# Router logits from unnormalised residual sums, joined attention keys and two more expert tiles in a three-layer decoder kernel

## The chip, the core and the metric

The kernel runs on one core of a Trainium2 chip, as one launch. The metric is the device time of one execution in microseconds, as the median of the runs shown. The engines are named as in the profile: PE is TensorE's matrix product and PEld its load of weights, DVE is VectorE, ACT is ScalarE, POOL is GpSimd and SP is SyncE, which here only issues DMAs.

## The reference, cut to what matters

Two layers of a first block are followed by one layer of a second block; the change touches the first block alone. It has 512 latent tokens and 256 context tokens of width 1024. One layer, cut to the lines that the change computes in another way:

```python
def layer_norm(x, g, b):
    mu = mean(x); var = mean((x - mu)**2)
    return (x - mu) * rsqrt(var + 1e-6) * g + b
def modulate(x, shift, scale):
    return layer_norm(x) * (1 + scale) + shift

# window attention, per block i of 128 queries: key blocks i-1, i, i+1 (banded), the 256 context keys, a sink
s = concat([where(band, q @ k_window, -1e30), q @ k_context, sink])
o = softmax(s) @ concat([v_window, v_context])
...
x = layer_norm(ALPHA * x + g1 * (o @ w_out), ln1_g, ln1_b)
h2 = modulate(x, sh2, sc2)
x = layer_norm(ALPHA * x + g2 * ec_moe(h2, ...), ln2_g, ln2_b)

def ec_moe(h, w_router, w_gate, w_up, w_down):      # 16 experts, each takes its best 2*n/16 tokens
    aff = softmax(h @ w_router)
    g, idx = top_k(aff.T, cap)
    ye = (silu(xs @ w_gate) * (xs @ w_up)) @ w_down * g     # xs = h[idx]
```

In layer 0 the context tokens go through the same steps with weights of modulation of their own; in layer 1 (`last`) they only serve as keys.

## The kernel before, in words

All products are float32. Many are made exact enough by splitting an operand into a high part (`fp32r`) and a low part; those run as three or two products. A router product or a transpose runs as plain float32, and each of its matmul calls is two instructions on TensorE.

A layer has these stages. **Projections and convolution** (`gemm`, L433 on). **Attention** (L587 to L730): `units` yields 4 + 4 neighbourhood units (`unit_b`) and 16 window units (`unit_a`, 4 pairs of heads `g` by 4 query blocks `i`), and in layer 0 also context units (`unit_c`); `pipeline` lays the back half of one unit beside the front half of the next. `unit_a` (L644) makes the scores of two heads in one PSUM tile `S_` with `qk` (L601), which is one product with the high and one with the low part of the keys: the block before (128 columns), the context (256), then this block and the next (128 or 256). So for `i` of 1 and 2 a unit has 12 products, of which 4 have 128 columns; for `i` = 3 it has 12, of which 8 have 128; for `i` = 0 it has 8 of 256. `softmax` (L624) reads the scores with the mask `band`, and `finish` transposes and multiplies with the values.

**Output projection and routing** (L733 to L868). First come loads on SP's queue: residual rows `xn`, gates `g`, norm vectors `lng` and `lnb`, router weights `wr`. Then `wrs` = router weights times (1 + scale), and the **setup products** `lg` of the shift with `wr` (L765), 8 calls for each of the two kinds of tokens in layer 0 and 8 in layer 1. `token_tile(t)` (L805) is a generator for 128 tokens, with these steps: four halves of the output product (12 matmuls each), where VectorE adds the residual (L800, L801); the first norm (`ln_affine`, in place) and the second norm to `z2` with its store to `zd`; 8 transposes of `z2` (L833) to `ht`; 8 router calls `lg` (L838), L842 to L848 the softmax; the transpose `tk` (L851) into the row of affinities; and after tile 3 `topk` of the latents (L885 on, VectorE). Tiles 0 to 3 are latents, 4 and 5 (layer 0 alone) context. The loop at L859 interleaves them by hand: in round `u` it steps tiles `(u, u-2, u, u, u-1, u, u-1, u-2)`. From `u` = 4 on TensorE's instructions are held in that order (`pin`); elsewhere a planner at build time with a cost model orders each engine's instructions, earlier ones in the program first.

**Experts** (`moe`, L955 on). 192 weight tiles of 128 by 2048 (1 MB each) per layer stream through a ring: `RIGHT` tiles `mr` in memory that is free early, `RING` = 4 tiles `r` (also used by the output projection) and `MRING` tiles `m`. That makes 12 in layer 0 and 16 in layer 1. A load waits until the tile that it replaces has been read. Of the first use of the ring, loads 6 to 11 in layer 0 and 14 and 15 in layer 1 are held behind the first gathers on POOL's queue (L985 to L989). `gather` (L997) fetches an expert pair's tokens by an indirect DMA from `zd`, transposes and modulates them to `xt`. In layer 0 `product0` runs the latent half of the first gate product, within it `topk` and `gather` for the context, then the context half.

Of the kernel before, what the change touches and what calls it, by code (L numbers as in the profile page):

```python
# [11 lines left out]
F32R = mybir.dt.float32r  # L12
# [3 lines left out]
OP = mybir.AluOpType  # L16
AX = mybir.AxisListType
# [14 lines left out]
RIGHT = (1, 3)  # L32
# [28 lines left out]
class K:  # L61
# [179 lines left out]
    def layer(self, l):  # L241
# [25 lines left out]
        band = self.t(kvp, [P, 640], tag="band")  # L267
# [70 lines left out]
        else:  # L338
# [238 lines left out]
        ML = self.t(mixp, [P, KC, 768], F32R, tag="lo")  # L577
        self.MH, self.ML = MH, ML
# [63 lines left out]
        zero = band[:, 128:384]  # L642

        def unit_a(g, i, qs):  # L644

            c0, c1 = (256 if i == 0 else 128), (640 if i == 3 else 768)
            n = c1 - c0
            vt = ([i - 1] if i else []) + [4, 5, i] + ([i + 1] if i < 3 else [])
            pt = []
            for s in range(2):  # L650
                S_ = self.t(ps, [P, 1024], tag="S")
                if i:
                    qk(S_, qs[s], s, i * P, KHA, KLA, 128, (i - 1) * P, P)
                qk(S_, qs[s], s, i * P, KHA, KLA, 256, 512, 256)
                qk(S_, qs[s], s, i * P, KHA, KLA, 512, i * P, P if i == 3 else 2 * P)
                p = self.t(ap_, [P, 769], tag=f"p{s}", bufs=3)
                softmax(p, [(S_[:, c0:c1], band[:, c0 - 128 : c1 - 128], slice(0, n))], n, s, g)
# [94 lines left out]
        nc.sync.dma_start(wr, A["w_r"][l])  # L752
        aff = self.sT.rearrange("p k s -> p (k s)")
# [4 lines left out]

        wrs, rb = [], []
        for s in range(1 if last else 2):  # L760
            w = self.t(ecp, [P, KC, NE], tag=f"wrs{s}", bufs=1)
            nc.vector.tensor_tensor(w, wr, mt[:, s, 32:40].unsqueeze(2).broadcast_to([P, KC, NE]), op=OP.mult)
# [42 lines left out]
        def token_tile(t):  # L805
# [8 lines left out]
            x = XN[:, t, :]  # L814
            self.ln_affine(x, s2, lng, lnb, sm, z2, self.t(ps, [P, D], tag="junk", bufs=1), sx)
# [13 lines left out]
            ht = self.t(ecp, [P, KC, P], tag="ht")  # L829
            for k0 in (0, 4):  # L830
                tp = self.t(ps, [P, 512], tag="tr")
                for k in range(k0, k0 + 4):
                    pin(nc.tensor.transpose(tp[:, (k - k0) * P : (k - k0 + 1) * P], z2[:, k * P : (k + 1) * P], self.ident))  # L833
                (nc.vector.tensor_copy if k0 else nc.scalar.copy)(ht[:, k0 : k0 + 4, :].rearrange("p k f -> p (k f)"), tp)
            yield
            lg = self.t(ps, [P, NE], tag="lg", bufs=1)
# [4 lines left out]
            g = self.t(sm, [P, NE], tag="rg")  # L841
            nc.vector.tensor_tensor_reduce(out=g, in0=lg, in1=rb[s], scale=1.0, scalar=-3.0e38, op0=OP.add, op1=OP.max, accum_out=mx)  # L842
# [112 lines left out]
    def moe(self, l):  # L955
# [21 lines left out]
        def load(src):  # L977
# [7 lines left out]
            if (right + RING + 1, 14)[l] <= n < right + RING + xr:  # L985
# [122 lines left out]
        def up(p):  # L1108
# [9 lines left out]
            ht = self.t(mp, [P, KC, P], tag="hT")  # L1118
# [14 lines left out]
        def down(p):  # L1133
# [813 lines left out]
def constants():  # L1947
# [11 lines left out]
    C["bandm"] = np.concatenate([np.where(k >= q, 0.0, NEG), np.zeros((P, 384)), np.where(k <= q, 0.0, NEG)], 1).astype(np.float32)  # L1959
# [28 lines left out]
def layout(I):  # L1988
# [13 lines left out]
    H["ln_vec"] = np.stack([I["ln1_g"], I["ln1_b"], I["ln2_g"], I["ln2_b"]], 1)  # L2002
    H["w_r"] = c(I["w_router"].reshape(2, KC // 2, P, 2, NE).transpose(0, 2, 1, 3, 4).reshape(2, P, KC, NE))
# [55 lines left out]
```

## Time and profile before

| | us |
|---|---|
| median of 3 runs (2538.52 to 2540.21) | 2538.67 |
| the profiled execution | 2537.64 |
| its span, first to last instruction | 2535.9 |
| layer 0: attention, from about | 210 to 355 |
| layer 0: output projection and routing | 355 to 486 |
| layer 0: experts in full flow | 486 to 1016 |
| layer 1: attention, from about | 1205 to 1315 |
| layer 1: output projection and routing | 1315 to 1411 |
| layer 1: experts in full flow | 1411 to 1866 |
| second block | 1866 to 2536 |

The stages overlap a little; the borders are those at which the timelines change hands. A timeline row gives the start, the duration, the engine, the line of the kernel, the operation, output and inputs by name, the shape and the count, and in brackets for how long the engine had been idle and what ended that. L97 is the helper of all matmuls. A matmul's duration holds its passage through the array, so that the cost of one in a row of them is read from start to start. In the table of stages the granted clock of TensorE is a share of full speed (1.00 is 2.4 GHz, 0.50 is 1.2 GHz) and DMA is the mean busy share of 16 DMA engines.

### The profile page before, as it was taken

Reading aid. Unit: us, or ns where it says so; the run is one execution under the profiler, and the core shown is the slowest. Engines: PE = TensorE matmul, PEld = TensorE weight load, DVE = VectorE, ACT = ScalarE, POOL = GpSimd, SP = SyncE. Lnnn points to the kernel's source line nnn. Section 1 sums busy time; section 2 is a strip of 40 time slices with the busy share of each in tenths; the row PEclk is TensorE's granted clock in tenths of the full one; section 3 lists DMA queues with packets and bytes.
Section 4 is the critical chain, followed back from the end, with each engine's and each line's share of the span. In section 5 each row is a group of like instructions: output and inputs, shape, how many; then the busy total and the mean of one; then the engine's idle time right before and its main releaser. Section 6 shows DMA issues by size and latency. Waiting matters only on the chain. (4 is left out here: it accounts for less than half of the span.)

```text
span 2535.9 us, 36633 instructions
## 1 busy us (share of the span) xinstructions
PE 2379.5 (94%) x14806; PEld 1454.1 (57%) x14806; DVE 1080.2 (43%) x2379; ACT 701.5 (28%) x1398; POOL 450.6 (18%) x628
## 2 busy tenths in 40 slices
PE   6999899899999999699897899999989989999999
PEld 3776778333333333377776333333357878888887
DVE  6957766311011100685866112221157676423232
ACT  3225643100000000542752100000043375322221
POOL 4013422111011111311430000000033332101100
PEclk9999899899999999789998899999999999999999
DMA  9445032899999999543224999999953302123220
GB/s 355 147 158 193 1 134 99 322 409 406 397 375 383 374 392 391 187 173 130 79 93 193 375 423 422 424 423 423 424 230 123 105 18 93 67 83 111 105 84 33
DMA packets 96537, 593.20 MB, mean 234 GB/s; under 512 B 12912, under 2 KB 13936, under 8 KB 31600
## 3 DMA queue, kind: packets, MB, share of 16 engines
q1 hardware_dynamic: 84240, 549.62, 54.7%
q0 software_dynamic: 8384, 30.68, 3.7%
q10 hardware_dynamic: 3744, 10.56, 1.1%
q8 instruction: 116, 1.90, 0.3%
q14 instruction: 53, 0.43, 0.0%
HBM read 571.68 MB, written 19.14 MB: 233 GB/s over the span
## 5 line engine op out<-in xcount | busy, mean ns | idle before, releaser
L97 PE MATMUL mm<-m,xt 128*32 128x512 f32 (+1 forms) x2536 | 412.8, 595 | 0.0
L97 PEld LDWEIGHTS mm<-m,xt 128*32 128x32 f32 (+1 forms) x2536 | 126.8, 115 | 216.5 <-issue 212.7
L97 PE MATMUL mm<-r,xt 128*32 128x512 f32 (+1 forms) x1128 | 238.7, 598 | 0.0
L97 PE MATMUL mm<-m,hT 128*32 128x512 f32 (+1 forms) x792 | 174.8, 595 | 6.1 <-DMA m<-w_down 6.1
L97 PE MATMUL mm<-mr,xt 128*32 128x512 f32 (+1 forms) x432 | 138.6, 615 | 0.2 <-ACT xt L1015 0.2
L1123 ACT COPY hT<-tr 128x512 f32<-128x512 f32 x16 | 9.4, 587 | 446.4 <-PE tr L1122 446.4
L97 PEld LDWEIGHTS mm<-r,xt 128*32 128x32 f32 (+1 forms) x1128 | 69.6, 117 | 90.4 <-issue 86.1
L97 PE MATMUL mm<-r,hT 128*32 128x512 f32 (+1 forms) x560 | 118.7, 594 | 1.7 <-DMA r<-w_down 1.7
L1114 DVE TENSOR_TENSOR sg<-sg,mm 128x512 f32<-128x512 f32 x32 | 22.0, 688 | 212.3 <-PE mm L97 142.7
L1013 DVE TENSOR_SCALAR xt<-tr,modT 128x128 f32<-128x128 f32 (+1 forms) x96 | 36.1, 388 | 170.4 <-ACT xt L1015 168.9
L521 DVE SCALAR_TENSOR_TENSOR acc<-hp,cw,acc 128x798 f32<-128x798 f32 (+1 forms) x120 | 106.2, 912 | 2.6 <-ACT acc L518 0.9
L97 PEld LDWEIGHTS mm<-m,hT 128*32 128x32 f32 (+1 forms) x792 | 54.9, 121 | 88.1 <-issue 69.0
L97 PE MATMUL po<-dl,rh 128*128 128x512 f32 x256 | 99.2, 390 | 1.4 <-DVE dl L1277 1.4
L1155 DVE SCALAR_TENSOR_TENSOR yd<-mm,gp,g 128x512 f32<-128x512 f32 x18 | 13.5, 751 | 204.1 <-PE mm L97 203.2
L1000 POOL DMA_INDIRECT gat<-zd,ip x24 | 23.1, 960 | 435.6 <-PE tr L1008 404.3
L97 PE MATMUL px<-HH,uh 128*128 128x512 f32 x256 | 99.8, 390 | 0.7 <-ACT HH L1847 0.7
L97 PE MATMUL px<-HH,ul 128*128 128x512 f32 x256 | 100.1, 391 | 0.0
L97 PE MATMUL pv<-ptT,VN 128*64 128x128 f32 x1360 | 96.1, 286 | 4.2 <-DVE lo L622 2.1
L97 PE MATMUL px<-HL,uh 128*128 128x512 f32 x256 | 100.0, 390 | 0.0
L97 PE MATMUL po<-dh,rh 128*128 128x512 f32 x256 | 98.7, 390 | 0.0
L97 PE MATMUL po<-dh,rl 128*128 128x512 f32 x256 | 98.6, 390 | 0.0
L640 POOL TENSOR_SCALAR p<-p,rl 128x768 f32<-128x768 f32 (+2 forms) x96 | 79.6, 833 | 104.1 <-DVE rl L639 95.0
(531 smaller groups left out, 5201.7 us busy)
## 6 DMA issues: line engine op xcount, KB each, us to landing
m<-w_gate SPq DMA_DIRECT2D x79, 1024.0 KB, 18.4
m<-w_down SPq DMA_DIRECT2D x71, 1024.0 KB, 18.8
m<-w_up SPq DMA_DIRECT2D x62, 1024.0 KB, 17.4
r<-w_mod SPq DMA_DIRECT2D x48, 1024.0 KB, 6.0
r<-w_down SPq DMA_DIRECT2D x41, 1024.0 KB, 17.3
r<-w_up SPq DMA_DIRECT2D x40, 1024.0 KB, 13.0
r<-w_gate SPq DMA_DIRECT2D x31, 1024.0 KB, 13.7
mr<-w_up SPq DMA_DIRECT2D x20, 1024.0 KB, 19.8
```

The lines of the kernel that those rows point to most:

```text
L97: return self.nc.tensor.matmul(out, lhsT, rhs, start=start, stop=stop)
L521: lambda t=t: nc.vector.scalar_tensor_tensor(out=dst, in0=hp[c][:, t : t + n], scalar=cw[:, c, t : t + 1], in1=dst, op0=OP.mult, op1=OP.add)
L640: nc.gpsimd.tensor_scalar(p[:, :n], p[:, :n], rl, 0.0, op0=OP.mult, op1=OP.add)
L1000: nc.gpsimd.indirect_dma_start(out=g[0:n], out_offset=None, in_=self.zd[l][s], in_offset=bass.IndirectOffsetOnAxis(ap=self.route[s][2][0:n ...
L1013: nc.vector.tensor_scalar(o, i, sc, sh, op0=OP.mult, op1=OP.add)
L1114: nc.vector.tensor_tensor(apart(sg[:, c]), apart(sg[:, c]), paired(ux[n]), op=OP.mult)
L1123: (nc.vector.tensor_copy if k0 else nc.scalar.copy)(ht[:, k0 : k0 + 4, :].rearrange("p k s -> p (k s)"), tp)
L1155: nc.vector.scalar_tensor_tensor(out=y, in0=d, scalar=gp[:, p : p + 1], in1=G2[0][:, c], op0=OP.mult, op1=OP.mult)
```

## The change

- `unit_a` makes the scores of the window's blocks in one product of up to 384 columns instead of two, with the context's beside them in the other PSUM bank; `band` and the order of the values follow.
- The token tiles transpose the residual sums `XN` (step 5, ahead of the first norm) instead of `z2`. The router multiplies them with `w1` = `wr` (1 + scale) gain, and the two means and two inverse deviations enter on VectorE as four operations of 128 by 16 on the logits. For that the setup makes four vectors instead of one: 24 calls instead of 8 for each kind of tokens, with a new load `lnT` (64 bytes for each partition).
- The order in a round is `(u, u-2, u-1, u, u-1, u, u, u-2)`.
- Layer 1's ring has five `mr` tiles instead of three, 18 in all. All its loads are on SP's queue. The room comes from single buffers for `gat`, `hT`, `oh` and the split output weights in layer 1, from split weights laid into the unused end of `MH` and `ML`, and from `h` in `QA`.

```diff
-RIGHT = (1, 3)
+RIGHT = (1, 5)
...
         nc.vector.scalar_tensor_tensor(out=x, in0=tmp, scalar=rs, in1=b, op0=OP.mult, op1=OP.add, accum_out=o)
+        return nm, rs
...
-                    h = self.t(lnp, [P, 512], tag="h")
+                    h = QA[k % 2]
...
+        if last:
+            MH, ML = (x.rearrange("p k f -> p (k f)") for x in (MH, ML))
+            spare = MH[:, KC * W : KC * 768], ML[:, KC * W : KC * 768]
+            MH, ML = (x[:, 0 : KC * W].rearrange("p (k f) -> p k f", k=KC) for x in (MH, ML))
...
-            c0, c1 = (256 if i == 0 else 128), (640 if i == 3 else 768)
-            n = c1 - c0
-            vt = ([i - 1] if i else []) + [4, 5, i] + ([i + 1] if i < 3 else [])
+            w = list(range(max(0, i - 1), min(4, i + 2)))
+            vt = w + [4, 5] if i == 0 else [4, 5] + w
+            n = len(vt) * P
+            cc, cw_, cm = (512, 256, 384) if i == 0 else (256, 512, 0)
...
-                if i:
-                    qk(S_, qs[s], s, i * P, KHA, KLA, 128, (i - 1) * P, P)
-                qk(S_, qs[s], s, i * P, KHA, KLA, 256, 512, 256)
-                qk(S_, qs[s], s, i * P, KHA, KLA, 512, i * P, P if i == 3 else 2 * P)
+                qk(S_, qs[s], s, i * P, KHA, KLA, cc, 512, 256)
+                qk(S_, qs[s], s, i * P, KHA, KLA, cw_, w[0] * P, len(w) * P)
...
+        lnT = self.t(ecp, [P, 2, KC], tag="lnT", bufs=1)
+        nc.sync.dma_start(lnT, A["ln_T"][l])
...
-            lg = self.t(ps, [P, NE], tag="lg", bufs=1)
-            for k in range(KC):
-                self.mm(lg, mt[:, s, 24 + k : 25 + k].broadcast_to([P, P]), wr[:, k, :], k == 0, k == KC - 1)
+            nc.vector.tensor_tensor(w1, w0, lnT[:, 0, :].unsqueeze(2).broadcast_to([P, KC, NE]), op=OP.mult)
+            lg = self.t(ps, [P, 4 * NE], tag="lg", bufs=1)
+            for o, n, lh, rh in (
+                (0, 2, lambda k: one, w), (2, 1, lambda k: lnT[:, 1, k : k + 1], w0), (3, 1, lambda k: mt[:, s, 24 + k : 25 + k], wr),
+            ):
+                for k in range(KC):
+                    self.mm(lg[:, o * NE : (o + n) * NE], lh(k).broadcast_to([P, P]), rh[:, k, :], k == 0, k == KC - 1)
...
-            if i < 3:
-                wh = self.t(ecp, [P, 2048], F32R, tag="woh")
-                wl = self.t(ecp, [P, 2048], F32R, tag="wol")
+            if last and i == 1:
+                wh, wl = spare
+            elif i < 3:
+                wh, wl = (self.t(ecp, [P, 2048], F32R, tag=n, bufs=1 if last else 2) for n in ("woh", "wol"))
...
             yield from product(t, 1, s2)
+            yield
+            x = XN[:, t, :]
+            xt = x.rearrange("p (a k b) -> p a b k", b=2, k=P)
+            ht = self.t(ecp, [P, KC, P], tag="ht", bufs=1)
+            for k0 in (0, 4):
+                tp = self.t(ps, [P, 512], tag="tr")
+                for k in range(k0, k0 + 4):
+                    pin(nc.tensor.transpose(tp[:, (k - k0) * P : (k - k0 + 1) * P], xt[:, k // 2, k % 2, :], self.ident))
+                (nc.vector.tensor_copy if k0 else nc.scalar.copy)(ht[:, k0 : k0 + 4, :].rearrange("p k f -> p (k f)"), tp)
...
-            self.ln_affine(x, s2, lng, lnb, sm, z2, self.t(ps, [P, D], tag="junk", bufs=1), sx)
+            nm1, rs1 = self.ln_affine(x, s2, lng, lnb, sm, z2, self.t(ps, [P, D], tag="junk", bufs=1), sx)
...
-                    pin(nc.tensor.transpose(tp[:, (k - k0) * P : (k - k0 + 1) * P], z2[:, k * P : (k + 1) * P], self.ident))
...
+            cW, cG, cB, cS = rb[s]
+            g = self.t(sm, [P, NE], tag="rg")
+            nc.vector.scalar_tensor_tensor(out=g, in0=cG, scalar=nm1, in1=lg, op0=OP.mult, op1=OP.add)
+            nc.vector.scalar_tensor_tensor(out=g, in0=g, scalar=rs1, in1=cB, op0=OP.mult, op1=OP.add)
+            nc.vector.scalar_tensor_tensor(out=g, in0=cW, scalar=nm, in1=g, op0=OP.mult, op1=OP.add)
+            nc.vector.scalar_tensor_tensor(out=g, in0=g, scalar=rs, in1=cS, op0=OP.mult, op1=OP.add)
...
-            nc.vector.tensor_tensor_reduce(out=g, in0=lg, in1=rb[s], scale=1.0, scalar=-3.0e38, op0=OP.add, op1=OP.max, accum_out=mx)
+            nc.vector.tensor_reduce(mx, g, axis=AX.X, op=OP.max)
...
-            for t in (u, u - 2, u, u, u - 1, u, u - 1, u - 2):
+            for t in (u, u - 2, u - 1, u, u - 1, u, u, u - 2):
...
-            if (right + RING + 1, 14)[l] <= n < right + RING + xr:
+            if not last and right + RING + 1 <= n < right + RING + xr:
...
-            g = self.t(mp, [P, D], tag=f"gat{s}", bufs=2 if last else 1)
+            g = self.t(mp, [P, D], tag=f"gat{s}", bufs=1)
...
-            ht = self.t(mp, [P, KC, P], tag="hT")
+            ht = self.t(mp, [P, KC, P], tag="hT", bufs=1 if last else 2)
...
-                oh = self.t(mp, [P, N], F32R, tag=f"oh{s}")
+                oh = self.t(mp, [P, N], F32R, tag=f"oh{s}", bufs=1 if last else 2)
```

## Rows read from the trace of the kernel before

**Rows 1.** Busy time by stage: us, PE, PEld, DVE, ACT, POOL, granted clock, DMA, GB/s.
```profile
215.00:355.00 140.00, 125.66 (x1180) 103.47 (x1180) 102.81 (x331) 90.64 (x227) 62.71 (x122) 0.95 0.15 60
355.00:440.00 85.00, 83.97 (x437) 69.52 (x433) 53.11 (x136) 24.91 (x41) 14.70 (x22) 1.00 0.44 162
...
486.00:1016.00 530.00, 529.71 (x4612) 176.76 (x4608) 63.28 (x116) 44.34 (x94) 72.55 (x62) 1.00 1.00 390
...
1315.00:1368.00 53.00, 52.21 (x262) 43.13 (x261) 31.63 (x69) 15.20 (x23) 4.04 (x7) 1.00 0.39 150
...
1411.00:1866.00 455.00, 440.01 (x1758) 171.28 (x1754) 90.46 (x151) 36.63 (x69) 5.12 (x8) 1.00 1.01 422
```

**Rows 2.** TensorE's timeline, layer 1's attention: start, us, engine, line, operation, tiles.
```profile
1274.88 0.36 PE L97 MATMUL S<-KHA,qs 128*128 128x256 f32 x1
...
1275.90 0.82 PE L614 MATMUL tr<-ident,p 128*128 128x128 f32 x6
...
1282.16 0.33 PE L97 MATMUL S<-KHA,qs 128*128 128x128 f32 x1
...
1283.66 1.03 PE L614 MATMUL tr<-ident,p 128*128 128x128 f32 x8
...
1286.28 0.31 PE L97 MATMUL S<-KHA,qs 128*128 128x128 f32 x1
...
1287.67 0.52 PE L614 MATMUL tr<-ident,p 128*128 128x128 f32 x3
```

**Rows 3.** TensorE's longest wait in layer 0's attention: us in total, times, longest.
```profile
PE S L97 <- DVE m L632: 7.0, 6, 3.2
```

**Rows 4.** TensorE's timeline, projection stage of layer 0 and then of layer 1.
```profile
376.32 1.85 PE L97 MATMUL lg<-wr,modT 128*128 128x16 f32 x16
378.03 0.48 PE L97 MATMUL po<-r,hi 128*128 128x512 f32 x1
...
1318.47 0.50 PE L97 MATMUL po<-woh,hi 128*128 128x512 f32 x1 [0.77 <-ACT woh L779]
```

**Rows 5.** SyncE's timeline, then VectorE's: the router weights in layer 0.
```profile
364.83 0.33 SPq L752 DMA_DIRECT2D wr<-w_r  x1
...
374.45 0.49 DVE L762 TENSOR_TENSOR wrs<-wr,modT 128x128 f32<-128x128 f32 x2 [0.33 <-DMA wr<-w_r]
```

**Rows 6.** Layer 0's routing, timelines of VectorE, GpSimd, TensorE and SyncE in turn.
```profile
431.47 0.41 DVE L885 MAX8 tkv<-sT 64x8 f32<-64x256 f32 x1
...
453.36 1.05 POOL L1000 DMA_INDIRECT gat<-zd,ip  x1 [0.30 <-issue]
...
469.85 0.95 POOL L1000 DMA_INDIRECT gat<-zd,ip  x1 [4.14 <-DVE gp L922]
...
479.79 1.06 PE L97 MATMUL mm<-mr,xt 128*32 128x512 f32 x1 [0.24 <-ACT xt L1015]
...
485.93 0.33 SPq L989 DMA_DIRECT2D mr<-w_up  x1
```

**Rows 7.** Layer 1's last token tile, VectorE's timeline.
```profile
1369.03 0.08 DVE L801 DVE_READ_ACCUMULATOR xn<-xn,ytmp 128x1 f32 x1
...
1375.73 0.16 DVE L818 TENSOR_TENSOR nb<-nm,rs 128x1 f32<-128x1 f32 x1 [0.66 <-POOL rs L226]
...
1382.25 0.17 DVE L842 CUSTOM_DVE_ANT_0 rg<-lg,rb 128x16 f32<-128x16 f32 x1 [2.73 <-PE lg L97]
...
1384.32 0.42 DVE L885 MAX8 tkv<-sT 64x8 f32<-64x256 f32 x1
```

**Rows 8.** Layer 1's first gather and first reused tile, GpSimd's and SyncE's timelines.
```profile
1399.02 1.09 POOL L1000 DMA_INDIRECT gat<-zd,ip  x1 [23.32 <-DVE oh L1148]
...
1410.37 0.98 SPq L989 DMA_DIRECT2D mr<-w_gate  x2
```

**Rows 9.** Gathers among the DMA issues of two stretches: count, median us to landing.
```profile
gat<-zd,ip POOLq DMA_INDIRECT x4, 6.0
...
gat<-zd,ip POOLq DMA_INDIRECT x12, 8.4
```

More of the change, by code (lines that the diff above doesn't have):

```diff
@@ L266, in layer @@
         nc.gpsimd.tensor_scalar(vec[:, 1:3, :], vec[:, 1:3, :], 0.5, 0.0, op0=OP.mult, op1=OP.add)
-        band = self.t(kvp, [P, 640], tag="band")
+        band = self.t(kvp, [P, 896], tag="band")
         colm = self.t(kvp, [P, 64], tag="colm")
@@ L640, in softmax @@
             nc.gpsimd.tensor_scalar(p[:, :n], p[:, :n], rl, 0.0, op0=OP.mult, op1=OP.add)
-        zero = band[:, 128:384]
+        zero = band[:, 0:256]
         def unit_a(g, i, qs):
-            c0, c1 = (256 if i == 0 else 128), (640 if i == 3 else 768)
-            n = c1 - c0
-            vt = ([i - 1] if i else []) + [4, 5, i] + ([i + 1] if i < 3 else [])
+            w = list(range(max(0, i - 1), min(4, i + 2)))
+            vt = w + [4, 5] if i == 0 else [4, 5] + w
+            n = len(vt) * P
+            cc, cw_, cm = (512, 256, 384) if i == 0 else (256, 512, 0)
             pt = []
@@ L651, in unit_a @@
                 S_ = self.t(ps, [P, 1024], tag="S")
-                if i:
-                    qk(S_, qs[s], s, i * P, KHA, KLA, 128, (i - 1) * P, P)
-                qk(S_, qs[s], s, i * P, KHA, KLA, 256, 512, 256)
-                qk(S_, qs[s], s, i * P, KHA, KLA, 512, i * P, P if i == 3 else 2 * P)
+                qk(S_, qs[s], s, i * P, KHA, KLA, cc, 512, 256)
+                qk(S_, qs[s], s, i * P, KHA, KLA, cw_, w[0] * P, len(w) * P)
                 p = self.t(ap_, [P, 769], tag=f"p{s}", bufs=3)
-                softmax(p, [(S_[:, c0:c1], band[:, c0 - 128 : c1 - 128], slice(0, n))], n, s, g)
+                softmax(p, [(S_[:, 256 : 256 + n], band[:, cm : cm + n], slice(0, n))], n, s, g)
                 pt.append(p)
@@ L752, in layer @@
         nc.sync.dma_start(wr, A["w_r"][l])
+        lnT = self.t(ecp, [P, 2, KC], tag="lnT", bufs=1)
+        nc.sync.dma_start(lnT, A["ln_T"][l])
+        one = self.t(ecp, [P, 1], tag="one", bufs=1)
+        nc.gpsimd.memset(one, 1.0)
         aff = self.sT.rearrange("p k s -> p (k s)")
@@ L760, in layer @@
         for s in range(1 if last else 2):
-            w = self.t(ecp, [P, KC, NE], tag=f"wrs{s}", bufs=1)
-            nc.vector.tensor_tensor(w, wr, mt[:, s, 32:40].unsqueeze(2).broadcast_to([P, KC, NE]), op=OP.mult)
-            lg = self.t(ps, [P, NE], tag="lg", bufs=1)
-            for k in range(KC):
-                self.mm(lg, mt[:, s, 24 + k : 25 + k].broadcast_to([P, P]), wr[:, k, :], k == 0, k == KC - 1)
-            b = self.t(ecp, [P, NE], tag=f"rb{s}", bufs=1)
+            w = self.t(ecp, [P, KC, 2 * NE], tag=f"wrs{s}", bufs=1)
+            w0, w1 = w[:, :, 0:NE], w[:, :, NE : 2 * NE]
+            nc.vector.tensor_tensor(w0, wr, mt[:, s, 32:40].unsqueeze(2).broadcast_to([P, KC, NE]), op=OP.mult)
+            nc.vector.tensor_tensor(w1, w0, lnT[:, 0, :].unsqueeze(2).broadcast_to([P, KC, NE]), op=OP.mult)
[5 more added lines that the diff above has]
+                    self.mm(lg[:, o * NE : (o + n) * NE], lh(k).broadcast_to([P, P]), rh[:, k, :], k == 0, k == KC - 1)
+            b = self.t(ecp, [P, 4 * NE], tag=f"rb{s}", bufs=1)
             nc.vector.tensor_copy(b, lg)
-            wrs.append(w)
-            rb.append(b)
+            wrs.append(w1)
+            rb.append([b[:, i * NE : (i + 1) * NE] for i in range(4)])
         for i in range(1, 4):
             w = self.load(A["w_out_t"][l, i].rearrange("p k f -> p (k f)"))
-            if i < 3:
-                wh = self.t(ecp, [P, 2048], F32R, tag="woh")
-                wl = self.t(ecp, [P, 2048], F32R, tag="wol")
+            if last and i == 1:
+                wh, wl = spare
+            elif i < 3:
+                wh, wl = (self.t(ecp, [P, 2048], F32R, tag=n, bufs=1 if last else 2) for n in ("woh", "wol"))
             else:
@@ L811, in token_tile @@
             yield from product(t, 1, s2)
+            yield
[7 more added lines that the diff above has]
+                (nc.vector.tensor_copy if k0 else nc.scalar.copy)(ht[:, k0 : k0 + 4, :].rearrange("p k f -> p (k f)"), tp)
             z2 = self.t(ecp, [P, D], tag="z2")
             sx = self.t(sm, [P, 1], tag="sx")
-            x = XN[:, t, :]
-            self.ln_affine(x, s2, lng, lnb, sm, z2, self.t(ps, [P, D], tag="junk", bufs=1), sx)
+            nm1, rs1 = self.ln_affine(x, s2, lng, lnb, sm, z2, self.t(ps, [P, D], tag="junk", bufs=1), sx)
             nm, rs = self.moments(x, sx, sm, self.t(ps, [P, D], tag="junk", bufs=1))
@@ L828, in token_tile @@
             yield
[L829 to L832, printed above, removed]
-                    pin(nc.tensor.transpose(tp[:, (k - k0) * P : (k - k0 + 1) * P], z2[:, k * P : (k + 1) * P], self.ident))
-                (nc.vector.tensor_copy if k0 else nc.scalar.copy)(ht[:, k0 : k0 + 4, :].rearrange("p k f -> p (k f)"), tp)
-            yield
-            lg = self.t(ps, [P, NE], tag="lg", bufs=1)
+            lg = self.t(ps, [P, 4 * NE], tag="lg", bufs=1)[:, 0:NE]
             for k in range(KC):
                 pin(self.mm(lg, ht[:, k, :], wrs[s][:, k, :], k == 0, k == KC - 1))
+            cW, cG, cB, cS = rb[s]
[4 more added lines that the diff above has]
+            nc.vector.scalar_tensor_tensor(out=g, in0=g, scalar=rs, in1=cS, op0=OP.mult, op1=OP.add)
             mx = self.t(sm, [P, 1], tag="rmx")
             nm = self.t(sm, [P, 1], tag="rnm")
-            g = self.t(sm, [P, NE], tag="rg")
-            nc.vector.tensor_tensor_reduce(out=g, in0=lg, in1=rb[s], scale=1.0, scalar=-3.0e38, op0=OP.add, op1=OP.max, accum_out=mx)
+            nc.vector.tensor_reduce(mx, g, axis=AX.X, op=OP.max)
             nc.vector.tensor_scalar_mul(nm, mx, -1.0)
@@ L1958, in constants @@
     q, k = np.arange(P)[:, None], np.arange(P)[None, :]
-    C["bandm"] = np.concatenate([np.where(k >= q, 0.0, NEG), np.zeros((P, 384)), np.where(k <= q, 0.0, NEG)], 1).astype(np.float32)
+    z = np.zeros((P, P))
+    C["bandm"] = np.concatenate([z, z, np.where(k >= q, 0.0, NEG), z, np.where(k <= q, 0.0, NEG), z, z], 1).astype(np.float32)
     qc, kc = np.arange(P)[:, None] % 64, np.arange(64)[None, :]
@@ L2002, in layout @@
     H["ln_vec"] = np.stack([I["ln1_g"], I["ln1_b"], I["ln2_g"], I["ln2_b"]], 1)
+    lt = np.stack([I["ln1_g"], I["ln1_b"]], 1)
+    H["ln_T"] = c(lt.reshape(2, 2, KC // 2, P, 2).transpose(0, 3, 1, 2, 4).reshape(2, P, 2, KC))
     H["w_r"] = c(I["w_router"].reshape(2, KC // 2, P, 2, NE).transpose(0, 2, 1, 3, 4).reshape(2, P, KC, NE))
```

## The prediction, made before the changed kernel was run

> **What bounds the kernel now.** I read the table of stages first, for what limits each stretch; then the timelines at the borders between stages, for what the next one waits for. In the experts' stretches the DMA engines are full, at a share of 1.00 in layer 0 and 1.01 at 422 GB/s in layer 1 [rows 1]. There the bytes still to come when the ring starts to turn set the end, and work saved on any engine is worth nothing; but whatever starts the ring earlier, or has put more bytes into memory by then, moves the end. In the output projections the bound is TensorE, busy 83.97 of 85 us and 52.21 of 53 at full clock [rows 1]. Between them lies the routing, a chain of latencies over all engines. Attention is mixed: TensorE is busy 125.66 of 140 us and VectorE 102.81 [rows 1], and the longest wait is of score products for VectorE to empty a score tile, 7.0 us in six waits [rows 3].
>
> So four terms count: TensorE's time in attention, its time in the projection, the routing's chain, and the tiles fetched ahead. What the second block does is unchanged.
>
> **Joined keys.** A unit with three blocks of keys holds TensorE from 1282.16 to 1283.66, 1.50 us for 12 products; the one with 8 narrow products from 1286.28 to 1287.67, 1.39 us; one of 8 products of 256 columns from 1274.88 to 1275.90, so 0.128 us each [rows 2]. After, the first kind has 4 of 256 and 4 of 384 columns. No row shows 384 here; between 0.128 us (no dearer than 256) and 0.192 (in proportion to columns) I take the middle, 0.16: a narrow product costs (1.50 - 8 x 0.128) / 4 = 0.12, nearly what twice the columns do, so columns alone don't set the price, and above 256 I can't tell when they begin to. That is 4 x 0.128 + 4 x 0.16 = 1.15, saving 0.35 us; the last kind becomes 8 of 256, 1.02, saving 0.37. Four pairs of heads, two units of the first kind and one of the second, two layers: 8 x (0.70 + 0.37) = 8.6 us. What reaches the end lies between 0 (VectorE sets the pace) and all of it. The units around these rows follow each other on TensorE without a gap, but at the changes of heads VectorE is late [rows 3]; I take 0.65, or **-5.6 us**, half in each layer.
>
> The Trainium skill's page "TensorE: Matmul & The Clock Gate" (section "Part 2: What happens when you issue a matmul") holds that throughput is "purely `N cycles`", one column a cycle. By that, joining saves next to nothing, as the columns stay the same. The trace speaks against it at this size: the 12 products of 1.50 us have 2560 columns, the 8 of 1.02 us have 2048, and the 12 of 1.39 us only 2048 too [rows 2], so that equal columns cost 0.37 us more in 12 products than in 8.
>
> **Setup products.** Each kind of tokens had 8 calls, 16 instructions, from 376.32 to 378.03: 1.71 us, 0.107 each [rows 4]. It gets 24 calls, so 32 instructions more, 3.42 us; those of the first vector are 32 columns wide instead of 16, which I cost at nothing, as even 128 columns cost about this much. Layer 0 has two kinds: **+6.84 us**; layer 1 **+3.42**. They lie in the stretch where TensorE has no gap to hide them [rows 1], so all of it arrives at the last projection product. The split weights laid into spare memory can be made before attention's memory is free; that takes away a stall of 0.77 us in layer 1 [rows 4]: **-0.77**. The planner could put the products elsewhere in the stretch, but not out of it, as `wr` lands only after it has begun.
>
> **Router in layer 1.** Before, the last tile's sum is ready at 1369.03 + 0.08, `nb` of the second norm at 1375.73, the logits at 1382.25 and topk at 1384.32 [rows 7]: 15.2 us. After, transposes and router products run beside the two norms. Logits then need the second deviation (at 1375.7, 6.6 us after the sum), wait on VectorE for `nb` and half of `z2` (0.9 us, as from 1375.73 on), two of the four new operations (0.17 each by L842's row), one more for the maximum (0.15), and then the 2.07 us from L842 to topk [rows 7]: 10.1 us, **-5.1**. The first norm's second pass now waits for the transposes, since it overwrites what they read; queued behind it on VectorE are the next half's residual sums, and the next product waits for those. The transposes come a half product earlier in the order, so I cost that at 0, at most 1 us per layer.
>
> **Routing in layer 0.** Here the reordering doesn't help: tile 3's `tk` is held behind the first half of tile 5, with the same work ahead of it as before plus the 6.84 us. So topk, at 431.47 before, starts that much later, and the first gather, at 453.36, as well [rows 6]. Only tile 5, the second context tile, has its chain shortened by some 5 us; but VectorE is in the latents' topk until then. The ring turns at 485.93, after the context products at 479.79, whose gather was issued at 469.85 and lay 9 us behind the six tiles on POOL's queue [rows 6]. Those tiles follow the first gather, which is late. So the ring's start moves by between +1.8 (6.84 less 5) and +6.84; nearer the latter: **+5.5 us** for layer 0's projection and routing together.
>
> **Two more tiles.** 2 x 1.049 MB at 422 GB/s [rows 1] is **-4.97 us** of DMA time moved to before 1368, where the DMA engines are at 0.39 [rows 1]; the two extra loads go out there and nobody waits behind them. Tiles 14 to 17 now go through SP's queue beside the gather, not after it. The gather took 6.0 us in the median around here and 8.4 within the full flow of layer 0 [rows 9]: between 0 and +2.4, taken at **+1.5**, as the queue is full only in part. In layer 1 the ring turned at 1410.37 after a gather issued at 1399.02 [rows 8]; it moves by 3.42 - 0.77 - 5.1 + 1.5 = -0.95 and has two tiles less to fetch. Single buffers for `gat`, `hT`, `oh`: cost nothing, the DMA engines hide them; if those ever waited, the cost would be a gather's 6 us once. `lnT`, the wider `band`, `h` in `QA`: nothing.
>
> **Sum.** -5.6 + 5.5 - 0.95 - 4.97 = -6.0 us. The profiled execution took 2537.64, so 2531.6; the median of before is 1.0 higher, and the forecast for the median is **2532.7**, 0.24% less. About 0.2%, 5.1 us, is what a measurement of this kernel can tell from no change: faster is below 2533.6, slower above 2543.8.
>
> **Rivals.** *Joining saves nothing* (chance 0.18): VectorE sets attention's pace, or columns alone count. For it: VectorE's waits [rows 3]; against it: rows 2. Time 2532.7 + 5.6 = 2538.3, no change. The Trainium skill's rule above is the second of these causes. *The new load stalls TensorE* (0.13), the slow side: `wr`, issued at 364.83, was used on landing at 374.45, 9.6 us later [rows 5], and TensorE wanted its products at 376.32 [rows 4]. `lnT` is queued behind it, and in layer 0 everything behind the setup products stands still in order until it lands; up to another 9.6 us. It decides the sign once the stall is over 6 us; with 9.6 the time is 2542.3. Against it: it is small and directly behind `wr`. *The two tiles don't come early* (0.12), the change not doing what it says: their memory could be freed only after routing. Then 2532.7 + 5.0 = 2537.7. *More than forecast* (0.12): all of the keys' 8.6 us and layer 0 at +1.8 give 2532.7 - 3.0 - 3.7 = 2526.0.
>
> **How the numbers follow.** The forecast has 0.45. Its own range is 2527 to 2538, from the shares of the keys (2.9 us more or 5.6 less) and layer 0's +1.8 to +6.84. Faster: two thirds of it (0.31), the last rival (0.12) and a part of the others (0.09), 0.52. Slower: half and more of the stall (0.08) and 0.06 for terms at their bad ends together, 0.14. The rest, 0.34, is the same. The range from 2523 to 2543 takes in the rivals and leaves out some 0.2.
>
> **What the profile would show.** Keys: units of `unit_a` 0.3 to 0.4 us shorter on TensorE and attention some 2 to 3 us shorter in each layer; wrong if it keeps its 110 us in layer 1. Setup: 48 instructions `lg` per kind of tokens in 5.1 us. Layer 0: from the end of attention to the first reused tile on SP's queue 4 to 7 us longer. Layer 1: from the last sum to topk some 10 us, five `mr` loads before the projection ends, and DMA full from a point that has 174 tiles left instead of 176. It is wrong if TensorE waits for `lnT`, or if the routing of layer 0 isn't longer.

## The result, and the profile after

The changed kernel took 2556.12 us as the median of 5 runs (2549.78 to 2562.49), against 2540.21 for the kernel before in the runs beside it: a ratio of 1.0058 (95% interval 1.0045 to 1.0072), 15 us slower by the ratio, 15.9 by the medians. The forecast was 2532.7, faster, with 2523 to 2543 as the range: both the sign and the range were wrong. The profiled execution took 2557.57 us, its span is 2555.8, 19.9 longer than that of the profiled execution before. Where they lie is read from the same marks in both timelines; the first reused tile is the first load of the ring that has to wait until a tile has been read, and with it the ring turns:

| from ... to ... | before | after | difference |
|---|---|---|---|
| start to layer 0's first score product | 212.29 | 213.88 | +1.6 |
| to layer 0's first projection product | 142.85 | 140.94 | -1.9 |
| to its last projection product | 84.19 | 99.34 | **+15.2** |
| to the first gather | 14.03 | 14.81 | +0.8 |
| to the first reused tile | 32.57 | 32.91 | +0.3 |
| to layer 1's first projection product | 828.50 | 827.22 | -1.3 |
| to its last projection product | 52.74 | 62.83 | **+10.1** |
| to topk | 17.15 | 11.93 | -5.2 |
| to the first gather | 14.70 | 14.72 | 0.0 |
| to the gather's transposes | 4.46 | 8.90 | **+4.4** |
| to the first reused tile | 6.89 | 8.11 | +1.2 |
| to the second block's first load | 452.31 | 448.33 | -4.0 |
| to the end | 673.2 | 671.9 | -1.3 |

The stages in the table of windows of the changed kernel, in the columns of [rows 1] (layer 0's projection, then layer 1's):

```profile
355.00:454.00 99.00, 98.18 (x507) 83.70 (x508) 58.16 (x159) 25.41 (x43) 14.76 (x21) 0.93 0.35 134
...
1329.00:1392.00 63.00, 63.00 (x318) 53.70 (x314) 30.91 (x81) 15.07 (x26) 3.67 (x8) 0.92 0.36 142
```

TensorE is busy through the whole of both projections, as before; but the granted clock, 1.00 there in [rows 1], is 0.93 and 0.92. The timeline of TensorE shows where, layer 0 first (the lines answer to [rows 4]):

```profile
376.26 1.87 PE L97 MATMUL lg<-wrs,one 128*128 128x32 f32 x16
...
377.96 1.94 PE L97 MATMUL lg<-wrs,lnT 128*128 128x16 f32 x16
...
379.75 3.58 PE L97 MATMUL lg<-wr,modT 128*128 128x16 f32 x16
...
383.16 0.77 PE L97 MATMUL po<-wol,hi 128*128 128x512 f32 x1
...
383.74 0.63 PE L97 MATMUL po<-woh,lo 128*128 128x512 f32 x1
...
387.13 0.39 PE L97 MATMUL po<-r,lo 128*128 128x512 f32 x1
...
389.44 1.87 PE L97 MATMUL lg<-wrs,one 128*128 128x32 f32 x16
...
391.15 1.94 PE L97 MATMUL lg<-wrs,lnT 128*128 128x16 f32 x16
...
392.93 3.15 PE L97 MATMUL lg<-wr,modT 128*128 128x16 f32 x16
...
395.92 1.20 PE L97 MATMUL po<-kb,hi 128*128 128x512 f32 x2
...
1339.36 1.87 PE L97 MATMUL lg<-wrs,one 128*128 128x32 f32 x16
1341.07 2.45 PE L97 MATMUL lg<-wrs,lnT 128*128 128x16 f32 x16
1343.35 3.57 PE L97 MATMUL lg<-wr,modT 128*128 128x16 f32 x16
1346.77 0.77 PE L97 MATMUL po<-r,lo 128*128 128x512 f32 x1
```

The first 16 instructions take 1.70 us, as forecast; the last 16 take 3.41, twice that (2.99 in the second setup of layer 0; in layer 1 the second 16 already take 2.28), and the product behind them holds TensorE for 0.4 us and more, where one takes 0.24 later on (387.13 to the next at 387.37). The windows over these stretches give the granted clock (last columns but two):

```profile
376.26:379.75 3.49, 3.49 (x34) 3.49 (x32) 2.09 (x9) 1.53 (x3) 0.56 (x1) 1.00 0.88 366
379.75:383.16 3.41, 3.41 (x18) 3.41 (x18) 0.26 (x1) 0.56 (x1) 1.70 (x2) 0.50 0.51 204
383.16:387.37 4.21, 4.21 (x13) 3.35 (x14) 0.23 (x1) 0.00 (x0) 0.00 (x0) 0.59 0.26 105
...
389.44:392.93 3.49, 3.49 (x33) 3.48 (x32) 1.89 (x5) 1.24 (x2) 0.56 (x1) 1.00 0.00 0
392.93:395.92 2.99, 2.99 (x18) 2.99 (x18) 0.00 (x0) 0.00 (x0) 0.00 (x0) 0.58 0.00 0
395.92:400.19 4.27, 4.27 (x16) 3.58 (x16) 0.23 (x1) 0.00 (x0) 0.00 (x0) 0.50 0.00 0
```

So the clock falls from 1.00 (2.4 GHz) to 0.50 (1.2 GHz) 3 to 4 us into each run of 48 narrow instructions. Read in slices of half a microsecond it falls at about 379.8, 393.4 and 1342.3 us, and it comes back only 3.4, 4.3 and 5.8 us after the run's end. TensorE was not idle for a moment, and at 389 to 396 us the DMA engines moved nothing, so neither a wait nor a transfer is needed for it.

Layer 1's end of the routing, VectorE's, SyncE's, GpSimd's and TensorE's timelines in the order of time (they answer to [rows 7, 8]):

```profile
1392.13 0.33 SPq L1012 DMA_DIRECT2D r<-w_gate  x1
1392.55 0.38 SPq L1012 DMA_DIRECT2D r<-w_up  x1
...
1393.72 0.08 DVE L817 DVE_READ_ACCUMULATOR xn<-xn,ytmp 128x1 f32 x1
...
1399.25 12.67 SPq L1012 DMA_DIRECT2D m<-w_up  x7
...
1403.86 0.42 DVE L908 MAX8 tkv<-sT 64x8 f32<-64x256 f32 x1
...
1411.96 0.90 SPq L1012 DMA_DIRECT2D m<-w_gate  x2
...
1418.58 1.10 POOL L1023 DMA_INDIRECT gat<-zd,ip  x1 [17.86 <-DVE oh L1171]
1427.48 1.97 PE L1031 MATMUL tr<-ident,gat 128*128 128x128 f32 x8 [10.99 <-DMA gat<-zd,ip]
...
1435.59 4.24 SPq L1012 DMA_DIRECT2D mr<-w_gate  x4
```

The gather's transposes on TensorE in the kernel before (its gather was issued at 1399.02, [rows 8]):

```profile
1403.48 1.97 PE L1008 MATMUL tr<-ident,gat 128*128 128x128 f32 x8 [6.56 <-DMA gat<-zd,ip]
```

From the last sum (1393.80) to topk are 10.06 us, 15.21 before. But eleven loads of 1 MB now stand on SP's queue between the last product and the gather, nine before, and the gather's rows come 8.90 us after its issue, 4.46 before.

### The profile page after: what moved, and what is told of

Read it like the earlier page. It is cut to its first block, busy times and chain, and to the rows that moved or that the text cites. A ratio compares the mean times of both kernels' runs of the same rounds, so it can differ in the third digit from the quotient of the medians.

```text
span 2555.8 us, 36684 instructions
## 1 busy us (share of the span) xinstructions
PE 2387.3 (93%) x14806; PEld 1461.0 (57%) x14806; DVE 1087.3 (43%) x2412; ACT 702.3 (27%) x1398; POOL 450.3 (18%) x628
## 5 line engine op out<-in xcount | busy, mean ns | idle before, releaser
L97 PE MATMUL mm<-m,xt 128*32 128x512 f32 (+1 forms) x2520 | 404.8, 596 | 0.1
L97 PE MATMUL mm<-r,xt 128*32 128x512 f32 (+1 forms) x1040 | 219.3, 596 | 0.0
L97 PE MATMUL mm<-m,hT 128*32 128x512 f32 (+1 forms) x688 | 146.6, 594 | 5.3 <-DMA m<-w_down 5.3
L97 PE MATMUL mm<-mr,xt 128*64 128x512 f32 (+1 forms) x536 | 148.4, 604 | 0.2 <-ACT xt L1038 0.2
L97 PE MATMUL mm<-r,hT 128*32 128x512 f32 (+1 forms) x616 | 138.0, 594 | 1.9 <-DMA r<-w_down 1.9
L97 PEld LDWEIGHTS mm<-r,xt 128*32 128x32 f32 (+1 forms) x1040 | 60.3, 115 | 82.2 <-issue 79.0
L97 PE MATMUL px<-hi,wh 128*128 128x512 f32 x224 | 92.0, 417 | 1.5 <-ACT hi L336 1.5
L97 PE MATMUL px<-lo,wh 128*128 128x512 f32 x224 | 89.9, 402 | 3.3 <-DVE lo L338 3.2
```

The source lines that it names most:

```text
L97: return self.nc.tensor.matmul(out, lhsT, rhs, start=start, stop=stop)
```

## The experiments

Ratios are to the kernel before in the runs beside them.

**E1. The four vectors in 8 calls.** VectorE makes the four products side by side and one vector of ones sums them.

```diff
-            w = self.t(ecp, [P, KC, 2 * NE], tag=f"wrs{s}", bufs=1)
+            w = self.t(ecp, [P, KC, 4 * NE], tag=f"wrs{s}", bufs=1)
+            w0, w1, w2, w3 = (w[:, :, i * NE : (i + 1) * NE] for i in range(4))
+            for o_, i_, m_ in ((w0, wr, mt[:, s, 32:40]), (w1, w0, lnT[:, 0, :]), (w2, w0, lnT[:, 1, :]), (w3, wr, mt[:, s, 24:32])):
+                nc.vector.tensor_tensor(o_, i_, m_.unsqueeze(2).broadcast_to([P, KC, NE]), op=OP.mult)
...
+            for k in range(KC):
+                self.mm(lg, one.broadcast_to([P, P]), w[:, k, :], k == 0, k == KC - 1)
```

> The changed kernel with the four setup vectors made in 8 calls of 64 columns (VectorE makes the four products with the constants side by side, one vector of ones sums them) instead of 24 calls of 16 and 32 columns; nothing else differs. Theory A, the clock: the run of 48 narrow instructions lets the granted clock fall to 0.50, so that they and some 4 us of projection products behind each run take twice as long. Without the run the clock holds 1.00: first to last projection product 99.3 -> about 85.7 us in layer 0, 62.8 -> about 54.5 in layer 1, the kernel 22 us less, about 2534. Rival B, the count: the calls cost 0.107 us per instruction and the low clock has another cause; 32 instructions less for each of three setups, 10.3 us less, about 2546, and the clock still falls. Rival C, the order: the new order of the tiles' steps and the moved transposes lengthen the projections; then no more than 3 us less, about 2553.

Measured: 2534.67 us, ratio 0.9977 (0.9966 to 0.9988). The projections take 85.77 and 54.49 us. In the timeline of E1 the setup of a kind of tokens is this:

```profile
374.49 1.89 PE L97 MATMUL lg<-wrs,one 128*128 128x64 f32 x16
```

and the windows hold the clock at 1.00 in it and behind it:

```profile
374.49:376.20 1.71, 1.71 (x18) 1.70 (x16) 1.30 (x4) 0.99 (x1) 0.00 (x0) 1.00 0.96 393
376.20:381.13 4.93, 4.93 (x24) 4.03 (x24) 3.21 (x9) 1.72 (x4) 2.26 (x3) 1.00 0.43 174
```

Theory A holds to the microsecond; B and C fall. This edit alone turns the loss into a gain of 5 to 6 us (5.8 by the ratio, 5.1 by the medians).

**E2. The 24 calls in three runs.** In the changed kernel the three groups of 8 calls of one kind are emitted after three successive half products, held in that order; `wr` and `lnT` are loaded ahead of the residual rows, and the results go to the tile `tk` instead of `lg`.

```diff
...
+                if held and i in (3, 5, 6):
+                    next(sets[u // 2], None)
...
```

> The changed kernel with all its 24 setup calls, but in three runs of 8 calls with a half product of the projection (some 2.8 us) between them, held in that order on TensorE; the router weights and the norm vector are loaded ahead of the residual rows so that they are there. Theory A: the clock holds 1.00, 0.107 us for each instruction: projection 92 to 93 us in layer 0, about 58 in layer 1, the kernel about 12 us less than changed, 2544. Rival: it is the number of these calls in the stage, not their being in one run, that lowers the clock: 0.50 is seen again, 99 and 63 us, about 2556.

Measured: 2544.67 us, ratio 1.0018 (1.0009 to 1.0027); projections 94.80 and 58.05 us. At one place in layer 0 the planner put a tile's router products directly behind a group, and there alone in the two projections the clock fell. The timeline of E2 at that place and, farther down, at another group with a product behind it:

```profile
393.21 1.87 PE L97 MATMUL tk<-wrs,one 128*128 128x32 f32 x16
394.91 2.07 PE L97 MATMUL lg<-wrs,ht 128*128 128x16 f32 x16
396.82 0.78 PE L97 MATMUL po<-woh,hi 128*128 128x512 f32 x1
...
401.13 1.85 PE L97 MATMUL tk<-wrs,lnT 128*128 128x16 f32 x16
402.84 0.71 PE L97 MATMUL po<-r,hi 128*128 128x512 f32 x2
```

and the windows of E2 over the end of the first, and over the second:

```profile
397.80:400.00 2.20, 2.20 (x7) 1.70 (x6) 1.19 (x6) 0.40 (x2) 0.61 (x1) 0.50 0.82 324
400.00:402.50 2.50, 2.50 (x19) 2.28 (x18) 0.00 (x0) 0.00 (x0) 0.00 (x0) 1.00 0.21 84
402.50:404.50 2.00, 2.00 (x12) 1.73 (x12) 0.00 (x0) 0.00 (x0) 0.00 (x0) 1.00 0.00 0
```

The same calls in the same number, apart, cost what was forecast for them: 10.0 us more than E1, where the count alone makes 10.3. And 32 narrow instructions in one run, 3.6 us, already brought 0.50. So it is the unbroken run that matters, not the number of calls in the stage.

**E3. The kernel before with 24 setup calls.**

```diff
...
-            for k in range(KC):
-                self.mm(lg, mt[:, s, 24 + k : 25 + k].broadcast_to([P, P]), wr[:, k, :], k == 0, k == KC - 1)
+            for o in (2, 1, 0):
+                for k in range(KC):
+                    self.mm(lg[:, o * NE : (o + 1) * NE], mt[:, s, 24 + k : 25 + k].broadcast_to([P, P]), wr[:, k, :], k == 0, k == KC - 1)
...
```

> The kernel before with its setup products of each kind of tokens made three times over (24 calls of 16 columns in one run; the two extra results go unused), nothing else. Theory A: the clock falls to 0.50 in the run here too, projection 84.2 -> 97 to 98 us in layer 0 and 52.7 -> 60 to 61 in layer 1, the kernel some 20 us more, about 2560. Rival B: 6.8 and 3.4 us more, about 2550, clock 1.00. Rival C: as B.

Measured: 2556.7 us, ratio 1.0078 (1.0063 to 1.0094); projections 97.68 and 57.89 us, so layer 1 came out 2 to 3 us shorter than expected. This one edit costs the kernel before 17 us by the medians, 20 by the ratio, more than the changed kernel's net loss; the projections lengthen by 13.5 and 5.2 us (changed kernel: 15.2 and 10.1), of which the count of the calls makes 6.8 and 3.4. Here the clock falls later, 4.4 to 5.5 us from the start of the run; in layer 1 only at its end, as the timeline and two windows of E3 show, so that what the clock costs there lies in the products behind the run:

```profile
1335.13 5.56 PE L97 MATMUL lg<-wr,modT 128*128 128x16 f32 x48
1340.53 0.78 PE L97 MATMUL po<-wol,hi 128*128 128x512 f32 x1
```

```profile
1338.00:1340.50 2.50, 2.50 (x23) 2.50 (x24) 0.44 (x2) 0.00 (x0) 0.00 (x0) 0.96 1.01 426
1340.50:1344.00 3.50, 3.50 (x10) 2.78 (x11) 0.17 (x1) 0.00 (x0) 0.00 (x0) 0.54 1.02 424
```

Some 1.5 of the 13.5 us come from another place, far from the setup. In layer 0 the clock also stands at 0.50 from about 425.5 to 429 us, behind eight transposes and the 16 router instructions of a token tile:

```profile
422.71 2.08 PE L97 MATMUL lg<-wrs,ht 128*128 128x16 f32 x16 [0.24 <-ACT ht L836]
...
426.59 1.05 PE L97 MATMUL po<-kb,hi 128*128 128x512 f32 x2
```

The profiles of E5 (408.4 to 411.7 us) and E9 (411.0 to 414.2) show the same behind the same steps, that of the kernel before does not (clock 1.00 throughout the projections).

**E4 and E10. Two tiles behind the gather.** E1, and loads 16 and 17 go out on GpSimd's queue.

```diff
-            if not last and right + RING + 1 <= n < right + RING + xr:
+            if (right + RING + 1, 16)[l] <= n < right + RING + xr:
```

> As the run with 8 setup calls, and the last two loads of layer 1's first ring turn (16 and 17) are held behind the first gathers on GpSimd's queue, as the kernel before held 14 and 15. Theory: the gather shares the DMA engines with the loads in front of it; it lands 4.5 us after its issue instead of 8.9, and the ring turns 4.4 us earlier: 4 us less than without the hold. Rival: the DMA engines' bytes set the start, and what is held comes later: 0, or up to 2.5 us more.

> The kernel with 8 setup calls and two held tiles once more, on the same chip as the run beside it and with the same runs of the kernel before. If its ratio to before, 0.9968 (0.9956 to 0.9981), holds on another chip, 8 us less than before; if that chip's share of the low clock in other stages sets it, anything between 4 and 13 us less.

Measured: 2530.85 us, ratio 0.9968 (0.9956 to 0.9981), 3.8 us less than E1 beside it; on another chip 2530.95 us, ratio 0.9953 (0.9939 to 0.9968). GpSimd's, TensorE's and SyncE's timelines of E4:

```profile
1390.36 1.09 POOL L1020 DMA_INDIRECT gat<-zd,ip  x1 [17.86 <-DVE oh L1168]
...
1395.82 1.97 PE L1028 MATMUL tr<-ident,gat 128*128 128x128 f32 x8 [7.56 <-DMA gat<-zd,ip]
...
1398.07 0.98 POOL L1020 DMA_INDIRECT gat<-zd,ip  x1 [6.62 <-PE tr L1028]
1399.05 1.17 POOL L1007 DMA_DIRECT2D m<-w_gate  x2
...
1405.01 7.19 SPq L1009 DMA_DIRECT2D mr<-w_gate  x5
```

The rows are there after 5.46 us, in E1 after 8.60 (1393.42 to 1402.02), and the ring turns 3.1 us earlier counted from the last product. The two rows of E1:

```profile
1393.42 1.09 POOL L1020 DMA_INDIRECT gat<-zd,ip  x1 [17.85 <-DVE oh L1168]
...
1402.02 1.97 PE L1028 MATMUL tr<-ident,gat 128*128 128x128 f32 x8 [10.69 <-DMA gat<-zd,ip]
```

So the gather did wait for the loads in front of it.

**E5. Joined keys alone**, as in the change's diff, on the kernel before.

```diff
...
-                if i:
-                    qk(S_, qs[s], s, i * P, KHA, KLA, 128, (i - 1) * P, P)
-                qk(S_, qs[s], s, i * P, KHA, KLA, 256, 512, 256)
-                qk(S_, qs[s], s, i * P, KHA, KLA, 512, i * P, P if i == 3 else 2 * P)
+                qk(S_, qs[s], s, i * P, KHA, KLA, cc, 512, 256)
+                qk(S_, qs[s], s, i * P, KHA, KLA, cw_, w[0] * P, len(w) * P)
...
```

> The kernel before with the joined keys alone (mask, order of the values and the split tile that makes room for the wider mask come with them). The prediction took 5.6 us off for it, out of 8.6 on TensorE. Theory A: what reaches the end is what the changed kernel's attention shows, 1.9 us in layer 0 and 0.8 in layer 1 between its first score and first projection product, because VectorE's softmax sets the pace; about 2.5 us less than before, 2537. Rival B, the prediction: 5.6 us less, 2534. Rival C: nothing, 2539.7.

Measured: 2538.1 against 2542.9 us, ratio 0.9983 (0.9973 to 0.9992): 4.3 us less by the ratio (4.8 by the medians), with 2 to 7 in the interval. A is not excluded, but B is as near, and C falls. Single profiles are no measure of it: layer 0's attention takes 136.9 us in this one and between 137.0 and 141.5 in those of the other kernels with the same attention.

**E6. Three right-hand tiles.** E4 with five tiles `mr` taken back to three, the hold to tiles 14 and 15, and the gathers' buffers to two (the other single buffers stay).

```diff
-RIGHT = (1, 5)
+RIGHT = (1, 3)
-            if (right + RING + 1, 16)[l] <= n < right + RING + xr:
+            if (right + RING + 1, 14)[l] <= n < right + RING + xr:
-            g = self.t(mp, [P, D], tag=f"gat{s}", bufs=1)
+            g = self.t(mp, [P, D], tag=f"gat{s}", bufs=2 if last else 1)
```

> As the run with 8 setup calls and two held tiles, but with three right-hand tiles in layer 1 as before, tiles 14 and 15 behind the first gathers, and the gathers' two buffers as before: the two extra tiles undone. Theory: they are worth their bytes, so without them 5.0 us more than with, about 2536, less up to 2 us because the second gather no longer holds up the tiles behind it. Rival: what they bring is already lost in the gather and the hold, 0 to 1 us more.

**E7. The held tiles ahead of the second gather.** E4, with loads 8 to 17 emitted in `product0`.

```diff
+            if last:
+                for i in range(10):
+                    early.append(weights(A["w_gate" if i > 7 else "w_up"], i // 8, i % 8 // 2, i % 2))
```

> As the run with 8 setup calls and two held tiles, but the two held tiles are issued between the first and the second gather. In that run they waited on GpSimd's queue behind the second gather, which waits for the single gather buffer, and the DMA engines stood at 0.08 from 1395 to 1400 us. Theory: that idle time is lost to the ring's later flow; with the tiles issued 7 us earlier the kernel is 3 to 5 us less, about 2527. Rival A: the tiles are wanted only later and the ring turns no earlier: 0. Rival B: they slow the first gather as in the changed kernel: up to 4 us more.

Measured, on one chip: E6 2533.85 us, ratio 0.9969 (0.9958 to 0.9981); E7 2529.74, ratio 0.9949 (0.9932 to 0.9966). With five tiles the experts run from the first reused tile to the second block in 448.4 us (E4, E7), with three in 452.6; from topk on it is 477.8 and 477.9 against 480.2, as the ring turns later after topk. So the two tiles are worth some 2 to 4 us once the gather is mended (2.4 in the profiles, 4.1 in the medians of E6 and E7), less than the 5 expected. E4 and E7 don't differ in their profiles, and the intervals of their ratios overlap; no gain of the earlier issue is shown, and rival A is the better supported. In E4 the DMA engines are full from 1401 us on, past the ring's turn at 1405.01; in E7 they are done with the held tiles at about 1405 and idle until the turn at 1407.36. So the pause in E4 costs nothing that the profiles show.

**E8. The old order of steps in layer 0**, on E7.

```diff
+            for t in (u, u - 2, u - 1, u, u - 1, u, u, u - 2) if last else (u, u - 2, u, u, u - 1, u, u - 1, u - 2):
```

> As the run with the held tiles ahead of the second gather, and layer 0 steps its token tiles in the order of before (layer 1 in the new one). Theory: the new order puts router products of one more tile ahead of layer 0's last projection product (85.8 us from the first with 8 setup calls, 84.2 before), and the first gather follows that product; with the old order 1.5 to 2.5 us less than without, clock unchanged. Rival: 0, since the same work lies ahead of the gather either way; or more, as the last tile's router comes later.

Measured: 2535.0 us, ratio 0.9963 (0.995 to 0.9976). Not less than E7; in the profile layer 0 takes 135.98 us from the first projection product to the first reused tile, against 131.52 in E7, and the first gather comes 16.5 us after the last product instead of 14.8. My theory falls. With the new router the new order looks the better one: the five profiles with the new router set up in 8 calls and the new order (E1, E4, E6, E7, E10) have 131.1 to 133.5 us and 14.8, though the intervals of the two ratios overlap.

**E9. The new router in layer 1 alone**, layer 0 with router, setup and order of before, on E4.

```diff
+            if last:
+                ht = turn(lambda k: xt[:, k // 2, k % 2, :])
...
+            if not last:
+                ht = turn(lambda k: z2[:, k * P : (k + 1) * P])
+                yield
```

> As the run with 8 setup calls and two held tiles, but layer 0 keeps the router, the setup (8 calls of 16 columns) and the order of steps of the kernel before; layer 1 has the new ones. From layer 0's first projection product to its first reused tile the kernel before took 130.8 us, with the joined keys alone 132.5, with the new router and 8 setup calls 133.5. Theory: the new router gains nothing in layer 0, as topk waits in the same place; 1 to 2.5 us less than the run repeated beside this one, and some 131 to 132 us in that stretch. Rival: the last context tile's shorter chain was worth something, 1 to 5 us more.

Measured beside E10: 2531.98 us, ratio 0.9959 (0.9946 to 0.9972), against 0.9953; the stretch in layer 0 takes 132.5 against 132.9 us. So no gain of the new router in layer 0 is seen, and all that it is shown to bring is in layer 1. Whether it costs 1 to 2 us there stays open: E9's stretch holds the low clock named under E3, worth some 1.5 us, and E10's does not, so that the profiles lean to the theory and the medians to the rival.

## Why the prediction was wrong

**The setup products** are the step that failed. It said "32 instructions more, 3.42 us" for each kind of tokens, from the 0.107 us of [rows 4]: a price read from a run of 16 instructions, carried over to one of 48. The count was right. In layer 0 the setups take 13.38 us (6.90 + 6.48) instead of 3.42: +9.96, of which 6.84 were forecast and 3.1 are the low clock; the slow products and transposes behind them add 1.6 and 2.1 (11 products in 4.21 us that take 2.6 at full clock; 6 products and 8 transposes in 4.27 us that take some 2.2). In layer 1 the setup takes 7.41 instead of 1.71 us, +5.7 against 3.42, and 13 products behind it 5.69 instead of 3.06, +2.6. So I had 10.3 us and 22.0 came, all but 3.3 of the 25.3 us by which the two projections lengthened; the 11.7 us of low clock that I had at nothing are half of the 23.4 between the forecast and the measured median. The step took the clock of [rows 1], 1.00, to hold whatever the run. E1 gives it back, E2 separates run from count, E3 shows it without the rest of the change. The Trainium skill's page "TensorE: Matmul & The Clock Gate" (section "Part 1: The HAM clock gate (the "warmup" mystery)") tells of the clock falling when TensorE idles; by that nothing would have happened here. The trace differs: the clock fell with TensorE busy 3.49 of 3.49 us ahead of it.

**The gather** was costed at +1.5 us and became +4.4, and the ring's turn behind it came another 1.2 later. I took the loads on SP's queue to be harmless, "the two extra loads go out there and nobody waits behind them", and did not ask what the shorter router chain runs into. Topk comes 5.2 us sooner after the last product, but eleven loads at some 2.5 us each fill the 26.7 us from there to the gather's issue. Most of what was saved in the chain was waited for in the queue. E4 gets 3.1 of it back. The 1.2 us were not tried by themselves. The single gather buffer, taken at nothing, may have a part in them: in E6, with two buffers and three tiles, the ring turns 7.34 us after the first transposes, in E1 and E4 9.19.

**The router in layer 1** was right: -5.1 forecast, 15.21 to 10.06 us measured. What I left out is its other side: the order now puts a tile more of transposes and router products ahead of the last product, 8 by 0.10 and 16 by 0.107, +2.5 us. Together with the setup's 5.7 and 2.6 and the spared stall of 0.77 that makes 10.0 of layer 1's +10.1. Net of it E1 has 66.53 us from the first projection product to topk, before 69.89.

**Joined keys**: the mechanism was right, a size was off. A product of 384 columns was taken at 0.16 us; in the changed kernel's timeline it is 0.175, from start to start, where one of 256 takes 0.118:

```profile
1294.75 0.34 PE L97 MATMUL S<-KHA,qs 128*128 128x384 f32 x1
1294.92 0.34 PE L97 MATMUL S<-KLA,qs 128*128 128x384 f32 x1
1295.10 0.28 PE L97 MATMUL S<-KHA,qs 128*128 128x256 f32 x1
1295.22 0.28 PE L97 MATMUL S<-KLA,qs 128*128 128x256 f32 x1
```

A unit with three blocks now takes 1.28 us (1294.41 to 1295.69), not 1.15, so that TensorE saves 8 x (2 x 0.22 + 0.36) = 6.4 us, not 8.6; of these E5 finds 4.3 at the end. That is near the share of 0.65 that I took, but the interval of 2 to 7 us leaves 0.3 to 1, so the share was a guess that the runs don't contradict. From 256 columns on the price goes with the columns: 0.118, 0.175 and, for 512, 0.235 us; a product of 128 columns at 0.12 us [rows 2] doesn't follow. The Trainium skill's page "TensorE: Matmul & The Clock Gate" (section "Part 2: What happens when you issue a matmul") has one column a cycle, by which 384 columns would take an estimated 0.16 us at 2.4 GHz. The trace has the same proportion above 256, but each product some 10% dearer.

**The two tiles** came early, all five `mr` loads at 1331.07, and shortened the experts by 4.0 us instead of 4.97. **The spare split weights** did what was said: no wait for `woh` is left in layer 1. **Layer 0's routing**: that the new router doesn't help there is what E9 supports; that the loss ahead of it reaches the ring's turn nearly whole holds too, only that it was 16.3 us (15.2 + 0.8 + 0.3) instead of 5.5.

**The rivals.** The slow side had a chance of 0.14 and rested on the wrong cause: in the changed kernel's profile TensorE never waits for `lnT`. That setup calls cost more than their count was not among the rivals. E4 is at 2530.9, near the forecast of 2532.7, but by other terms, so by luck: it has neither the setups' cost nor most of the gather's.

## What to carry to other kernels

A price read from a short burst holds for a burst of that length: when a change makes a run of small products three times as long, ask what the granted clock does in it and behind it, and break the run up or fold the calls together. Where constants are sums of products, one call of 64 columns against a vector of ones did the work of three of 16 to 32. And when a chain is shortened, look at what has to be finished by its new end: here the loads that it used to hide.

## What the runs showed of the hardware

- Granted clock: it fell to 0.50 with TensorE busy all the time, 3 to 4 us into runs of 48 plain float32 instructions of 16 and 32 columns in the changed kernel, and 4.4 to 5.5 us from the start of such runs in E3. Runs of 16 such instructions by themselves, 1.7 us, left it at 1.00 (E1, E2). Eight transposes, a wait of 0.24 us and 16 router instructions, 3.2 us together, did so in the kernel before, but were followed by 0.50 at one place in each of the profiles of E3, E5 and E9. What sets the moment stays open, and no run here separates the few columns from the plain float32.
- Plain float32 calls cost the same at 16, 32 and 64 columns: 16 instructions in 1.7 us [rows 4], at 376.26 after, and in E1.
- An indirect gather behind full queues took 8.90 us from issue to use (8.60 in E1), 5.46 with two loads of 1 MB less in front of it (E4), and 4.46 in the kernel before, where the DMA engines were at 0.02 in the 2 us ahead of it.
- The changed kernel's runs lie 12.7 us apart, those of before beside them 2.7; the setups' share in this was not tried.
